# Rates' product of the SSD mixer in plain float32 on the two halves of the array, decay exponents finished on GpSimd, softplus on 128 columns

## The chip, the cores and the metric

The kernel runs on one core of one Trainium2 chip. The metric is the device time of one execution in microseconds, given as the median of several runs; a lower time is better.

## The reference, cut to what matters

The model is a trunk of two layers over 256 tokens of width 2048. Layer 0 mixes tokens with Mamba-2 (SSD), layer 1 with an RG-LRU; each is followed by a SwiGLU FFN and a gated per-layer embedding. The change lies in the SSD mixer of layer 0. Its projection gives, beside z and xBC, one rate per head (64 heads) and token, and the rates give the decays:

```
u = rms_norm(h, norm_mix)
z, xbc, dt = split(u @ in_proj, [4096, 10240])     # dt: the last 64 columns
dt = softplus(dt + dt_bias);  a = -exp(a_log)
a_cs = cumsum(dt * a) within each of the two chunks of 128 tokens
decay_in = exp(where(causal, a_cs[l] - a_cs[s], -inf))
y_diag = einsum(cb, decay_in, xs * dt)             # cb = C . B of a chunk
y_off: the same with the state that chunk 0 leaves for chunk 1
```

There are 8 groups of 8 heads. A head's decays are three 128x128 blocks: chunk 0 with itself, chunk 1 with itself, and chunk 1 against chunk 0 (from the later of whose tokens the state comes).

## The kernel before

**Panels.** Activations lie with features on partitions and the 256 tokens on the free dimension. A weight matrix is walked in panels of 512 output columns. For a panel, `panel` (L226 on) loads raw float32 weights, 512 KB a piece, into a pool of five buffers; `weights` makes of each piece a rounded part `hi` (a cast on ScalarE, L239) and the remainder `lo` (a subtraction on VectorE, L240), four buffers each. For each 128x128 block TensorE multiplies `hi` with 512 columns (the rounded activations and their remainder side by side, L268) and `lo` with 256 columns (L265). For a panel of four blocks the products go in rounds: 16 of `hi`, then 16 of `lo`; four rounds make a panel. All of this is in program order on each engine's own queue as the planner of the framework lays it out; an instruction that waits holds up all behind it on its engine.

**Side work.** After each 12 products `panel` takes one step of a generator in `post` and, by a credit (`pump`, 1.4 steps, 0.6 for two panels of B, 1.35 for the xs panels), one or so of a generator in `side`. Each `yield` ends such a step. So the number of yields sets beside which products a piece of side work is laid.

**The SSD mixer (L382 on)** takes panel 18 (part of C; beside it `load` brings h and scales it into the operands u, which do not yet hold the norm's factor), then the rates' product, panel 19, panels 16 and 17 (B), panels 8 to 15 (xs, one for each group of heads), panels 0 to 7 (z) and the output product. The norm's factor r of each token is made beside panel 19: `bc_part` squares the 16 blocks of h on ScalarE and adds them on VectorE into one accumulator (L176), and `rstd` sums it over partitions with tiny products (L187) and spreads it.

**The rates before.** The weights' 64 columns stand twice side by side in `w_dt`, as two pieces of 512 KB, and go through `panel` like any other, with one block (nb=1): 16 products of `hi` and 16 of `lo`, in which rows 64 to 127 repeat rows 0 to 63. `dt_part` (a side generator) then waits for r, scales, adds the bias, takes softplus (an exp on ScalarE and a series on VectorE) on 128x256, the running sums per chunk into `cs` (128x384: chunk 0, chunk 1 plus chunk 0's total, chunk 1), four transposes (L448), a copy of `cs` to a buffer `sums` in DRAM (96 KB), 29 copies of that row in DRAM (four DMAs, 2784 KB), and then `spread`: for each pair of heads one DMA of 384 KB that gives every partition the pair's running sums (L105; GpSimd masks the two diagonal blocks with affine_select, L403). `move` puts such a DMA on SyncE's queue behind the weight load that was issued last, `last_load`.

**Decays and outputs.** `decays(g)` multiplies B with C (L479, L480), copies that to `cm`, and takes for each head two exps on ScalarE (L88, e<-e,ncs) with minus the token's running sum as the bias, 256 and 128 columns; each pair of heads is then multiplied with `cm` on VectorE (L488). `group(g)` convolves xs, calls `spread` for the next group, takes the steps of `decays(g + 1)`, transposes xs (L507) and makes the outputs: for each head two plain float32 products with 64 weight columns, of 256 and 128 moving columns (L523, L525), heads alternating between rows 0 to 63 and rows 64 to 127 of the bank.

Of the kernel before, what the change touches and what calls it, by code (L numbers as in the profile page):

```python
# [27 lines left out]
COPY = 64 * 384 + 576  # L28
# [16 lines left out]
class Trunk:  # L45
# [120 lines left out]
    def square_add(self, acc, src, first, after=None):  # L166
        nc = self.nc
        q = acc if first else self.tmp.tile([P, T], F32, name="q", tag="q")
        i = nc.scalar.activation(q, src, AF.Square).ins  # L169
        if after is not None:  # L170
            self.tc.add_manual_dep(
                i, after.name,
                mybir.DependencyInfo(mybir.DependencyClass.NoSync, mybir.DependencyReason.DATA),
                reason="not before")
        if not first:
            nc.vector.tensor_tensor(acc, acc, q, ALU.add)  # L176
# [182 lines left out]
    def softplus(self, v, n):  # L359
# [9 lines left out]
        nc.vector.reciprocal(s, s)  # L369
        nc.vector.tensor_tensor(s, s, e, ALU.mult)  # L370
# [12 lines left out]
    def ssd_mixer(self, w_dt, w_in, w_out, load):  # L383
# [7 lines left out]

# [3 lines left out]
        def spread(g, j):  # L395


            e = es[g, j] = pool.tile([P, 2, 384], F32, name="e", tag="e", bufs=8)
            src = sums[0, (g * 8 + 2 * j) * 384:(g * 8 + 2 * j + 2) * 384]
            self.move(e.rearrange("p h c -> p (h c)"),  # L400
                      bass.AP(src.tensor, src.offset, [[COPY, 16], [2 * COPY, 8], [1, 768]]))
            for o in (0, 256):
                nc.gpsimd.affine_select(  # L403
                    out=e[:, :, o:o + P], in_=e[:, :, o:o + P], compare_op=ALU.is_ge, fill=-1e30,
                    base=0, pattern=[[0, 2], [1, P]], channel_multiplier=-1)
# [6 lines left out]
        def bc_part(n, ts, first=None):  # L412
            if first is not None:
                for i in range(0, KT, 4):
                    for k in range(i, i + 4):
                        self.norm_square(k, after=first)
                    yield
# [7 lines left out]
        def dt_part(t):  # L425
            while self.r is None:
                yield
            t = self.scaled(t, self.r)
            v = self.act.tile([P, T], F32, name="dt_v", tag="a")
            nc.vector.tensor_scalar(v, t, self.vec("dt_bias"), None, ALU.add)  # L430
            for dt in self.softplus(v, T):
                yield
# [3 lines left out]
            adt = self.act.tile([P, T], F32, name="adt", tag="a")  # L436
            nc.vector.tensor_scalar(adt, dt, a, None, ALU.mult)
            cs = self.act.tile([P, 384], F32, name="cs", tag="a")

            for c, o in ((0, 0), (1, 256)):  # L440
                nc.vector.tensor_tensor_scan(cs[:, o:o + P], self.ones, adt[:, c * P:(c + 1) * P],
                                             0.0, ALU.mult, ALU.add)
            nc.vector.tensor_scalar(cs[:, P:256], cs[:, 256:], cs[:, P - 1:P], None, ALU.add)
            for _ in range(6):
                yield
            b = self.bank()
            for i, src in enumerate((dt[:, :P], dt[:, P:], cs[:, :P], cs[:, 256:])):
                nc.tensor.transpose(b[:, i * P:(i + 1) * P], src, self.ident)  # L448
            dts = pool.tile([P, 2, P], F32, name="dts", tag="dts", bufs=1)
            ncs = pool.tile([P, 2, P], F32, name="ncs", tag="ncs", bufs=1)  # L450
            nc.vector.tensor_copy(dts, b[:, :256])
            nc.vector.tensor_scalar(ncs, b[:, 256:], -1.0, None, ALU.mult)
            self.dts, self.ncs = dts, ncs
            yield
            yield
            rows = sums[:, :64 * 384]
            self.move(rows[0].rearrange("(h c) -> h c", h=64), cs[:64])
            for _ in range(3):
                yield
            for n in range(1, NCOPY, 8):  # L460
                m = min(n + 8, NCOPY)
                self.move(rows[n:m].rearrange("n (a b) -> n a b", b=1024),
                          rows[0:1].rearrange("n (a b) -> n a b", b=1024).to_broadcast([m - n, 24, 1024]))
                yield
            for _ in range(8):
                yield
            for j in range(NB):
                spread(0, j)
                yield
# [4 lines left out]
        def decays(g):  # L474
# [4 lines left out]
            nc.tensor.matmul(b[:, :256], bt[:, :P], ct, start=True, stop=True, skip_group_check=True)  # L479
            nc.tensor.matmul(b[:, 256:384], bt[:, P:], ct[:, P:], start=False, stop=True, skip_group_check=True)  # L480
            cm = pool.tile([P, 384], F32, name="cm", tag="cm")
            nc.scalar.copy(cm, b[:, :384])
            for n in range(8):
                e, hh, hd = es[g, n // 2], n % 2, g * 8 + n
                self.table(e[:, hh, :256], e[:, hh, :256], AF.Exp, bias=self.ncs[:, 0, hd:hd + 1])
                self.table(e[:, hh, 256:], e[:, hh, 256:], AF.Exp, bias=self.ncs[:, 1, hd:hd + 1])
                if hh:
                    nc.vector.tensor_tensor(e, e, cm.unsqueeze(1).to_broadcast([P, 2, 384]), ALU.mult)  # L488
                yield

        def group(g, ts):
# [23 lines left out]
            def outputs(j):  # L515

                yb = self.bank()
                for i in (j, j + 1):
                    for hh in range(2):
                        e = es[g, i][:, hh, :]  # L520
                        ch = slice(i * P + hh * 64, i * P + hh * 64 + 64)
                        o = yb[hh * 64:hh * 64 + 64, (i - j) * T:(i - j + 1) * T]
                        nc.tensor.matmul(o, xdt[0][:, ch], e[:, :256], start=i == j, stop=False,  # L523
# [360 lines left out]
```

## Time and profile before

| | |
|---|---|
| median of 3 runs | 2684.91 us (2683.16 to 2685.52) |
| the profiled execution's own time | 2682.07 us |
| its span, first to last instruction | 2680.3 us |
| PE busy | 2648.2 us (99%) |
| DVE busy | 1822.4 us (68%) |
| ACT busy | 1501.7 us (56%) |
| POOL busy | 32.5 us (1%) |
| mean granted TensorE clock | 0.996 |
| moved by DMA | 510.77 MB, 191 GB/s |

PE is TensorE's products, PEld its weight loads, DVE VectorE, ACT ScalarE, POOL GpSimd, SP SyncE, on whose queue the DMAs are issued. Times count from the first instruction. "Idle before" in square brackets is the time for which an engine stood still before an instruction, with what released it. PEclk is TensorE's granted clock as a share of the full 2.4 GHz; 0.5 would be 1.2 GHz throughout.

### The profile page before, as it was taken

How to read it: one execution, taken by the hardware profiler on the slowest of the kernel's cores; microseconds unless marked ns; L12 is line 12 of the kernel's file. 1: busy time of each engine (PE TensorE's matmuls, PEld its weight loads, DVE VectorE, ACT ScalarE, POOL GpSimd, SP SyncE). 2: the span in 40 equal slices, each digit the busy share in tenths (PEclk: the TensorE clock that was granted, in tenths of full speed). 3: DMA queues.
4: the chain of work that ended last, by engine and by line, in shares of the span. 5: the costliest groups of instructions: out<-in, count | busy, mean ns of one | idle time of the engine just before them, and what ended most of it. 6: DMA issues, size and time to landing. Idle time of an engine off the chain costs nothing.

```text
span 2680.3 us, 40689 instructions
## 1 busy us (share of the span) xinstructions
PE 2648.2 (99%) x15346; PEld 2334.0 (87%) x15346; DVE 1822.4 (68%) x3066; ACT 1501.7 (56%) x2399; POOL 32.5 (1%) x70
## 2 busy tenths in 40 slices
PE   9899999999999999999999999999999999999998
PEld 7788888888888888888888888888888888888887
DVE  7888878855566655555666899977666555665667
ACT  7677755544444444444455678856444444444555
POOL 0011100000000000000000000000000000000000
PEclk9999999999999999999999999999999999999999
DMA  6767655555555555555655565555555555556553
GB/s 232 244 209 219 190 181 184 186 189 189 184 193 189 189 182 190 195 190 189 194 187 188 172 195 176 196 189 189 189 189 189 196 190 180 189 193 202 186 187 125
DMA packets 141915, 510.77 MB, mean 191 GB/s; under 512 B 15901, under 2 KB 16349, under 8 KB 141661
## 3 DMA queue, kind: packets, MB, share of 16 engines
q1 hardware_dynamic: 141719, 508.18, 57.9%
q8 instruction: 120, 1.97, 0.3%
q14 instruction: 76, 0.62, 0.1%
HBM read 505.92 MB, written 5.05 MB: 191 GB/s over the span
## 4 chain that ended last, share of the span: by engine, by line
PE 90%; DVE 6%; ACT 2%; issue 1%; DMA 1%; SPq 0%; DVEq 0%; ACTq 0%
PE bank L268 58%; PE bank L265 30%; DVE c L356 1%; DVE lo L240 1%; ACT hi L239 1%; DVE t L156 1%; DMA raw<-in_w_ssd_in_dram 1%; PE bank L523 1%; DVE t L163 1%; DVE xc L356 0%; PE bank L625 0%; ACT L88 0%; PE bank L525 0%; PE bank L507 0%; ACT s L153 0%
## 5 line engine op out<-in xcount | busy, mean ns | idle before, releaser
L268 PE MATMUL bank<-x,hi 128*128 128x512 f32 x7360 | 1771.7, 392 | 12.0 <-ACT hi L239 9.9
L268 PEld LDWEIGHTS bank<-x,hi 128*128 128x128 f32 x7360 | 1351.6, 189 | 277.4 <-ACT hi L239 12.7
L239 ACT CAST hi<-raw 128x1024 fp32r<-128x1024 f32 (+1 forms) x932 | 972.1, 1048 | 1031.6 <-PE bank L268 962.6
L240 DVE TENSOR_TENSOR lo<-raw,hi 128x1024 fp32r<-128x1024 f32 (+1 forms) x932 | 1107.2, 1220 | 503.4 <-issue 431.1
L265 PEld LDWEIGHTS bank<-x,lo 128*128 128x128 f32 x7360 | 949.5, 191 | 42.0 <-DVE lo L240 4.8
L265 PE MATMUL bank<-x,lo 128*128 128x256 f32 x7360 | 967.2, 283 | 4.4 <-DVE lo L240 4.4
L156 DVE TENSOR_TENSOR t<-bank,s 128x256 f32<-128x256 f32 x448 | 161.9, 418 | 291.3 <-ACT s L153 290.5
L153 ACT COPY s<-bank 128x256 f32<-128x256 f32 x496 | 160.3, 374 | 13.4 <-PE bank L265 4.8
L163 DVE TENSOR_TENSOR t<-t,r 128x256 f32<-128x256 f32 x216 | 83.2, 427 | 0.0
L356 DVE SCALAR_TENSOR_TENSOR c<-t,vecs,c 128x255 f32<-128x255 f32 (+1 forms) x144 | 63.1, 487 | 0.1
L145 ACT ACTIVATE x<-h,vecs 128x256 fp32r<-128x256 f32 x96 | 47.4, 501 | 17.0 <-DVE h L337 13.8
L88 ACT ACT_TABLE_LOAD x43 | 55.2, 1283 | 1.1 <-DVE c L356 0.3
L337 DVE TENSOR_TENSOR h<-h,t 128x256 f32<-128x256 f32 x144 | 54.2, 420 | 0.2
L146 DVE SCALAR_TENSOR_TENSOR x<-h,vecs,x 128x256 fp32r<-128x256 f32 x96 | 45.5, 480 | 5.9 <-ACT x L145 5.9
L88 ACT ACTIVATE e<-e,ncs 128x256 f32<-128x256 f32 (+1 forms) x128 | 45.3, 442 | 0.1
L176 DVE TENSOR_TENSOR acc<-acc,q 128x256 f32<-128x256 f32 x104 | 43.8, 421 | 2.2 <-ACT q L169 1.4
L169 ACT ACTIVATE q<-h 128x256 f32<-128x256 f32 x104 | 41.4, 405 | 4.7 <-DVE h L337 3.8
L88 ACT ACTIVATE sg<-t 128x256 f32<-128x256 f32 x88 | 32.3, 412 | 18.7 <-DVE t L163 18.7
L137 ACT CAST x<-t 128x256 fp32r<-128x256 f32 x88 | 31.8, 403 | 18.8 <-DVE t L717 18.8
L488 DVE TENSOR_TENSOR e<-e,cm 128x768 f32<-128x768 f32 x32 | 31.0, 970 | 12.6 <-ACT e L88 6.5
L403 POOL TENSOR_SCALAR_AFFINE_SELECT e<-e 128x256 f32<-128x256 f32 x64 | 31.8, 519 | 274.1 <-DMA e<-sums 236.7
L138 DVE TENSOR_TENSOR x<-t,x 128x256 fp32r<-128x256 f32 x88 | 33.3, 421 | 0.0
(121 smaller groups left out, 679.1 us busy)
## 6 DMA issues: line engine op xcount, KB each, us to landing
raw<-in_w_ffn_in_dram SPq DMA_DIRECT2D x352, 512.0 KB, 4.6
raw<-in_w_ffn_out_dram SPq DMA_DIRECT2D x176, 512.0 KB, 4.4
raw<-in_w_ssd_in_dram SPq DMA_DIRECT2D x158, 512.0 KB, 4.5
raw<-in_w_ssd_out_dram SPq DMA_DIRECT2D x64, 512.0 KB, 4.3
raw<-in_w_ple_gate_dram SPq DMA_DIRECT2D x64, 512.0 KB, 4.3
raw<-in_w_lru_in_dram SPq DMA_DIRECT2D x64, 512.0 KB, 4.2
raw<-in_w_lru_out_dram SPq DMA_DIRECT2D x32, 512.0 KB, 4.7
e<-sums SPq DMA_DIRECT2D x32, 384.0 KB, 6.0
```

Of the source, the lines that this page charges most:

```text
L88: i = self.nc.scalar.activation(out, in_, func, **kw).ins
L145: nc.scalar.activation(x[:, :T], src, AF.Copy, scale=w)
L146: nc.vector.scalar_tensor_tensor(x[:, T:], src, w, x[:, :T].bitcast(F32), ALU.mult, ALU.subtract)
L153: nc.scalar.copy(s, b[:, T:])
L156: nc.vector.tensor_tensor(t, b[:, :T], s, ALU.add)
L163: self.nc.vector.tensor_tensor(t, t, r, ALU.mult)
L239: self.last_hi = nc.scalar.copy(hi, src).ins
L240: nc.vector.tensor_tensor(lo, src, hi.bitcast(F32), ALU.subtract)
L265: self.last_product = nc.tensor.matmul(b[:, T:], wt, x[:, :T], start=False, stop=k == nk - 1, skip_group_check=True)
L268: self.last_product = nc.tensor.matmul(b, wt, x, start=k == 0, stop=False, skip_group_check=True)
L337: self.nc.vector.tensor_tensor(hb, hb, t, ALU.add)
L356: nc.vector.scalar_tensor_tensor(out[:, d:], t[:, :T - d], self.vec(cw, (3 - d) * ntap + i), out[:, d:], ALU.mult, ALU.add)
```

## The change

- The rates' product leaves `panel`. `rates` loads the 64 columns once (two pieces of 256 KB into tiles of the activations' pool), multiplies them with norm_mix on VectorE (128x512 each), and multiplies them in plain float32 with h itself, chunk 0 into rows 0 to 63 and chunk 1 into rows 64 to 127 of one bank. The bank is held until r is there.
- So all that follows has 128 columns in place of 256, softplus in more steps; the running sums of a chunk come out of one scan, three transposes take the place of four, and two DMAs (one for each chunk) put them in DRAM, 64 KB in all; the 29 copies are 1856 KB, in four DMAs that lie three steps apart.
- `spread` brings two pairs of heads with one DMA of 512 KB, and GpSimd then does three adds (128x512 each, one with the token's own running sum per block) and two masks of 128x512. There are two spreads for each group in place of four.
- `decays` takes one exp of 128x768 for each pair of heads, with no bias; the product with `cm` and the output products have the same sizes with other strides.
- The squares of the first norm go into two accumulators, of which GpSimd adds one (7 of the adds) and VectorE the other.

```diff
 def square_add(self, acc, src, first, after=None, adder=None):
...
+            (adder or nc.vector).tensor_tensor(acc, acc, q, ALU.add)
 # softplus: two more yields behind the reciprocal and in the series
-            if k == 9:
+            if k in (13, 9, 5):
                 yield
 # spread(g, j), now for j = 0 and 2
+            e = es[g, j // 2] = pool.tile([P, 3, 4, P], F32, name="e", tag="e", bufs=4)
+            n = g * 8 + 2 * j
+            src = sums[0, n * T:(n + 4) * T]
+            self.move(e[:, :2].rearrange("p m h c -> p (m h c)"),
+                      bass.AP(src.tensor, src.offset, [[COPY, 16], [2 * COPY, 8], [1, 4 * T]]))
+            add = lambda m: self.ncs[:, m, n:n + 4].unsqueeze(2).to_broadcast([P, 4, P])
+            nc.gpsimd.tensor_tensor(e[:, 2], e[:, 1], add(2), ALU.add)
+            for m in range(2):
+                nc.gpsimd.tensor_tensor(e[:, m], e[:, m], add(m), ALU.add)
                 nc.gpsimd.affine_select(
+                    out=e[:, m], in_=e[:, m], compare_op=ALU.is_ge, fill=-1e30,
+                    base=0, pattern=[[0, 4], [1, P]], channel_multiplier=-1)
+        def rates():
+            b = self.bank()
+            for i in range(2):
+                w = self.act.tile([P, 8, 64], F32, name="w_dt", tag="a")
+                nc.sync.dma_start(w, w_dt[:, i * 8:i * 8 + 8, :])
+                nc.vector.tensor_tensor(w, w, self.vecs[:, i * 8:i * 8 + 8].unsqueeze(2).to_broadcast([P, 8, 64]),
+                                        ALU.mult)
+                for k in range(8):
+                    for c in range(2):
+                        nc.tensor.matmul(b[c * 64:c * 64 + 64, :P], w[:, k, :],
+                                         self.h[:, i * 8 + k, c * P:(c + 1) * P],
+                                         start=i + k == 0, stop=i + k == 8, skip_group_check=True)
+            return b
 # dt_part(b)
+            for p, c in half:
+                nc.vector.tensor_tensor(v[p], b[p, :P], self.r[p, c], ALU.mult)
+            nc.vector.tensor_scalar(v, v, self.vec("dt_bias"), None, ALU.add)
+            for dt in self.softplus(v, P):
+                yield
...
+            nc.vector.tensor_tensor_scan(cs[:, 0, :], self.ones, adt, 0.0, ALU.mult, ALU.add)
+            nc.vector.tensor_scalar(cs[:64, 1, :], cs[:64, 0, :], -1.0, cs[:64, 0, P - 1:], ALU.mult, ALU.add)
+            for c in range(2):
+                self.move(sums[0, :64 * T].rearrange("(q c h l) -> c q h l", q=16, c=2, h=4)[c],
+                          cs[64 * c:64 * c + 64, 0, :])
+            for _ in range(4):
+                yield
...
             for n in range(1, NCOPY, 8):
+                for _ in range(3):
+                    yield
...
+            for j in (0, 2):
+                for _ in range(3):
+                    yield
                 spread(0, j)
 # decays(g)
-            for n in range(8):
-                e, hh, hd = es[g, n // 2], n % 2, g * 8 + n
-                self.table(e[:, hh, :256], e[:, hh, :256], AF.Exp, bias=self.ncs[:, 0, hd:hd + 1])
-                self.table(e[:, hh, 256:], e[:, hh, 256:], AF.Exp, bias=self.ncs[:, 1, hd:hd + 1])
+            for n in range(4):
+                e = es[g, n // 2][:, :, n % 2 * 2:n % 2 * 2 + 2, :]
+                self.table(e, e, AF.Exp)
+                nc.vector.tensor_tensor(e, e, cm.unsqueeze(2).to_broadcast([P, 3, 2, P]), ALU.mult)
                 yield
 # group(g)
-                if g < 7:
+                if g < 7 and j % 2 == 0:
                     spread(g + 1, j)
...
-            for n in range(5):
-                next(ahead, None)
-                yield
-            yield
+            for n in range(6):
+                if n % 2:
+                    next(ahead, None)
+                yield
 # ssd_mixer
-        self.side.append(dt_part(self.totals(self.panel(w_dt, u, kt=8, nb=1, post=False))[0]))
+        self.side.append(dt_part(rates()))
```

## Rows read from the trace of the kernel before

**Rows 1.** Busy time of each engine by stage: the stretch in us from the span's start and its length, then for each engine its busy time (and instructions), the granted clock, the DMA share and GB/s.
```profile
58.00:83.00 25.00, 20.61 (x111) 18.09 (x111) 23.34 (x50) 17.13 (x27) 0.00 (x0) 0.86 0.37 120
83.00:140.00 57.00, 52.80 (x292) 45.68 (x291) 45.26 (x73) 40.07 (x70) 10.13 (x16) 0.97 0.82 272
140.00:352.00 212.00, 209.78 (x1343) 182.42 (x1342) 183.16 (x297) 161.23 (x291) 21.66 (x48) 1.00 0.66 205
352.00:2667.00 2315.00, 2311.24 (x13314) 2041.25 (x13313) 1520.65 (x2550) 1241.13 (x1945) 0.00 (x0) 1.00 0.57 187
```

**Rows 2.** Timeline of TensorE's products from 30 to 77 us: start, duration, engine, line, operation, count, and the idle time before.
```profile
30.39 3.82 PE L268 MATMUL bank<-x,hi 128*128 128x512 f32 x16
...
35.96 3.82 PE L268 MATMUL bank<-x,hi 128*128 128x512 f32 x16
...
64.45 3.82 PE L268 MATMUL bank<-x,hi 128*128 128x512 f32 x16
72.67 3.78 PE L265 MATMUL bank<-x,lo 128*128 128x256 f32 x16 [4.39 <-DVE lo L240]
76.24 2.64 PE L268 MATMUL bank<-x,hi 128*128 128x512 f32 x9
```

**Rows 3.** Timeline of VectorE from 63 to 73 us, of which these are three.
```profile
63.05 1.75 DVE L369 RECIPROCAL sp<-sp 128x256 f32<-128x256 f32 x1
65.75 0.15 DVE L435 TENSOR_SCALAR a_neg<-a_neg 128x1 f32<-128x1 f32 x1 [0.95 <-ACT a_neg L88]
...
71.39 1.22 DVE L240 TENSOR_TENSOR lo<-raw,hi 128x1024 fp32r<-128x1024 f32 x1
```

**Rows 4.** Groups of instructions by line and shape, over the whole span: busy us, mean ns of one, idle before.
```profile
L403 POOL TENSOR_SCALAR_AFFINE_SELECT e<-e 128x256 f32<-128x256 f32 x64 | 31.8, 519 | 274.1 <-DMA e<-sums 236.7 <-DVE lo L240 25.9 <-DVE t L163 4.9
...
L88 ACT ACTIVATE e<-e,ncs 128x256 f32<-128x256 f32 x64 | 31.8, 497 | 0.1
...
L88 ACT ACTIVATE e<-e,ncs 128x128 f32<-128x128 f32 x64 | 24.8, 387 | 0.0
...
L375 DVE SCALAR_TENSOR_TENSOR sp<-sp,sp 128x256 f32<-128x256 f32 x7 | 3.0, 422 | 0.0
...
L369 DVE RECIPROCAL sp<-sp 128x256 f32<-128x256 f32 x1 | 1.7, 1747 | 0.0
...
L375 DVE SCALAR_TENSOR_TENSOR sp<-sp,sp 128x16 f32<-128x16 f32 x7 | 1.2, 173 | 0.2
...
masks.py:199 POOL TENSOR_SCALAR_AFFINE_SELECT ident<-ident 128x128 f32<-128x128 f32 x1 | 0.3, 292 | 0.1
L369 DVE RECIPROCAL sp<-sp 128x16 f32<-128x16 f32 x1 | 0.2, 248 | 0.0
```

**Rows 5.** Timeline of TensorE's products in the outputs of group 0: two of the four pairs of heads (each float32 product leaves two records).
```profile
159.11 0.65 PE L523 MATMUL bank<-e,xdt 128*64 128x256 f32 x4
...
159.76 0.65 PE L523 MATMUL bank<-e,xdt 128*64 128x256 f32 x4
```

**Rows 6.** Timeline of TensorE's products at the first norm's sum over partitions.
```profile
45.66 0.50 PE L187 MATMUL bank<-ones,acc 128*128 128x1 f32 x4
```

**Rows 7.** Timeline of SyncE's queue, on which DMAs are issued, from 84 to 104 us.
```profile
84.54 2.86 SPq L105 DMA_DIRECT2D sums<-sums  x4
87.93 4.32 SPq L231 DMA_DIRECT2D raw<-in_w_ssd_in_dram  x2
103.37 0.61 SPq L105 DMA_DIRECT2D e<-sums  x1
```

**Rows 8.** Timeline of ScalarE from 104 to 187 us, of which these are three.
```profile
104.60 1.05 ACT L239 CAST hi<-raw 128x1024 fp32r<-128x1024 f32 x1 [4.34 <-DMA raw<-in_w_ssd_in_dram]
...
128.71 4.95 ACT L88 ACTIVATE e<-e,ncs 128x256 f32<-128x256 f32 x14
...
181.07 5.65 ACT L88 ACTIVATE e<-e,ncs 128x256 f32<-128x256 f32 x16
```

**Rows 9.** Timeline of TensorE's products from 105 to 140 us.
```profile
105.70 3.96 PE L268 MATMUL bank<-x,hi 128*128 128x512 f32 x16 [0.58 <-ACT hi L239]
...
117.50 3.01 PE L268 MATMUL bank<-x,hi 128*128 128x512 f32 x12 [0.37 <-ACT hi L239]
120.36 0.59 PE L479 MATMUL bank<-bc,bc 128*128 128x256 f32 x2
...
120.93 1.17 PE L268 MATMUL bank<-x,hi 128*128 128x512 f32 x4
...
129.40 2.00 PE L268 MATMUL bank<-x,hi 128*128 128x512 f32 x8
134.65 3.38 PE L268 MATMUL bank<-x,hi 128*128 128x512 f32 x8 [3.25 <-ACT hi L239]
...
140.06 3.82 PE L268 MATMUL bank<-x,hi 128*128 128x512 f32 x16
```

**Rows 10.** All masks on GpSimd by their line: durations in ns (least/median/most), first and last start in us.
```profile
L403 POOL TENSOR_SCALAR_AFFINE_SELECT e<-e x64: 401/407/1384, 107.9 to 306.6; 128x256 f32<-128x256 f32 x64
```

**Rows 11.** Timeline of GpSimd: the masks of two pairs of heads, two masks each.
```profile
135.26 2.50 POOL L403 TENSOR_SCALAR_AFFINE_SELECT e<-e 128x256 f32<-128x256 f32 x2 [0.19 <-DMA e<-sums]
163.69 0.77 POOL L403 TENSOR_SCALAR_AFFINE_SELECT e<-e 128x256 f32<-128x256 f32 x2 [25.94 <-DVE lo L240]
```

**Rows 12.** Timeline of VectorE beside the first of the rows of GpSimd.
```profile
134.73 4.10 DVE L240 TENSOR_TENSOR lo<-raw,hi 128x1024 fp32r<-128x1024 f32 x3
```

More of the change, by code (lines that the diff above doesn't have):

```diff
@@ L164, in scaled, with square_add @@
         return t
-    def square_add(self, acc, src, first, after=None):
+    def square_add(self, acc, src, first, after=None, adder=None):
         nc = self.nc
@@ L413, in bc_part @@
             if first is not None:
-                for i in range(0, KT, 4):
-                    for k in range(i, i + 4):
-                        self.norm_square(k, after=first)
-                    yield
+                self.acc = [self.tmp.tile([P, T], F32, name="acc", tag="acc") for _ in range(2)]
+                for k in range(KT):
+                    self.square_add(self.acc[k % 2], self.h[:, k, :], k < 2, first, nc.gpsimd if k % 2 else None)
+                    if k % 4 == 3:
+                        yield
                 yield from self.norm_end()
@@ L423, in bc_part, with dt_part @@
                 yield
-        def dt_part(t):
+        def dt_part(b):
             while self.r is None:
                 yield
[L428 to L431, printed above, removed]
+            v = self.act.tile([P, P], F32, name="dt_v", tag="a")
+            half = [(slice(c * 64, c * 64 + 64), slice(c * P, c * P + P)) for c in range(2)]
+            for p, c in half:
+                nc.vector.tensor_tensor(v[p], b[p, :P], self.r[p, c], ALU.mult)
+            nc.vector.tensor_scalar(v, v, self.vec("dt_bias"), None, ALU.add)
+            for dt in self.softplus(v, P):
                 yield
@@ L435, in dt_part @@
             nc.vector.tensor_scalar(a, a, -1.0, None, ALU.mult)
-            adt = self.act.tile([P, T], F32, name="adt", tag="a")
+            adt = self.act.tile([P, P], F32, name="adt", tag="a")
             nc.vector.tensor_scalar(adt, dt, a, None, ALU.mult)
[L438 to L442, printed above, removed]
@@ L443, in dt_part @@
-            nc.vector.tensor_scalar(cs[:, P:256], cs[:, 256:], cs[:, P - 1:P], None, ALU.add)
-            for _ in range(6):
+            yield
+            cs = self.act.tile([P, 2, P], F32, name="cs", tag="a")
+            nc.vector.tensor_tensor_scan(cs[:, 0, :], self.ones, adt, 0.0, ALU.mult, ALU.add)
[3 more added lines that the diff above has]
+                          cs[64 * c:64 * c + 64, 0, :])
@@ L453, in dt_part @@
-            self.dts, self.ncs = dts, ncs
-            yield
[L455 to L459, printed above, removed]
+            nc.tensor.transpose(b[:, :P], dt, self.ident)
+            nc.tensor.transpose(b[:, P:2 * P], cs[:, 0, :], self.ident)
+            nc.tensor.transpose(b[:, 2 * P:2 * P + 64], cs[:64, 1, :], self.ident[:64, :64])
+            dts = pool.tile([P, 2, 64], F32, name="dts", tag="dts", bufs=1)
@@ L461, in dt_part @@
                 m = min(n + 8, NCOPY)
                 self.move(rows[n:m].rearrange("n (a b) -> n a b", b=1024),
[L463 to L467, printed above, removed]
+                          rows[0:1].rearrange("n (a b) -> n a b", b=1024).to_broadcast([m - n, 16, 1024]))
+            for j in (0, 2):
+                for _ in range(3):
+                    yield
```

43 lines of the change are left out of this document (16 added, 27 removed).

## The prediction

> **What bounds the kernel now.** I read the busy times by stage first. From 352 us to the end of the last products TensorE is busy 2311 of 2315 us at the full 2.4 GHz [rows 1]; nothing of the change lies there, and that part can neither give nor lose much. Before 352 us three stages fall short: from 58 to 83 us TensorE is busy 20.6 of 25 us at a mean clock of 0.86, from 83 to 140 us 52.8 of 57, from 140 to 352 us 209.8 of 212 [rows 1]. So the change can win in three ways: fewer columns streamed, fewer stops before 140 us, and the 2.2 us of idle after it. Then I read the timelines of TensorE, to price the stops in rounds. An undisturbed round, 16 hi products and 16 lo products, takes 5.57 us (35.96 less 30.39; that very round is the rates' product) [rows 2]. The round from 64.45 to 76.24 takes 11.79: 4.39 us of idle until VectorE has made lo, then a lo half that lasts 3.57 where an undisturbed one takes 1.9 or so, at the lower clock [rows 1, 2]. Loss 6.2 us. The round from 129.40 to 140.06 takes 10.66, with 3.25 us of idle until ScalarE has cast hi [rows 9]. Loss 5.1 us. Two smaller stops, 0.58 and 0.37, stand before hi at 105.70 and 117.50 [rows 9].
>
> **The change part by part.**
>
> *The rates' product.* Removed: one round, 5.57 us of TensorE [rows 2], with two casts and two subtractions. Added: 16 pairs of plain float32 products, 128 moving columns each, on the two halves. The nearest rows are the outputs, which have the same 64 weight columns: one pair of heads, 256 and 128 columns in each half, goes by in 0.65 us (159.76 less 159.11) [rows 5], so both halves together cost 0.65/3 = 0.217 us for 128 columns. The same 256 and 128 columns in float32 over the whole array, B's product with C, take 0.57 (120.93 less 120.36) [rows 9]. So the halves run side by side there; in turns they would take twice that. 16 x 0.217 = 3.5 us. Net -2.1 us. Upper bound: the halves take turns, because here the order alternates after every product and each brings new weights: 16 x 0.43 = 6.9 us, net +1.4. Lower bound -2.2. I take -2.1, for the outputs alternate after every second product already. The weights' scaling is two operations of 128x512 on VectorE, against two subtractions of twice that size, 1.22 us each [rows 3], now; it is due at 30 us, and its loads are half the bytes of those now, so I cost it at nothing; late, it would cost its own 2.4 us at most.
>
> *The first norm.* Two accumulators need four more records of the tiny product; four now take 0.50 us with the tail [rows 6]: +0.4. One transpose less: -0.1. The adds given to GpSimd take 7 x 0.42 us off VectorE where it does not stop TensorE; if GpSimd is late, r is late, but TensorE takes r only beside panel 19's end. The bank is held longer (from 30 us to r, some 53 us): panels 19 and 16 want eight, so panel 16's last bank waits if VectorE's scaling by r comes after 58 us. Up to +1, taken as 0.
>
> *Softplus and the stop at 72.67.* The lo that TensorE waits for starts at 71.39 on VectorE [rows 3], behind the reciprocal at 63.05, a wait of 0.95 us for ScalarE's a_neg, and five of the seven steps of the series. At 128 columns the reciprocal falls, on the line between its 16 and 256 column rows (248 and 1747 ns) [rows 4], to 0.95 us: -0.80. The series' step falls from 422 ns on the line to 173 at 16 columns to 0.29: -0.13 each, for five of these and some four of their kind -1.2. So lo is ready 2.0 us earlier with the order of VectorE's queue as it is, and idle falls to 2.4. Beyond that, the change puts three more step ends into softplus and one behind it, so that about half of the series is laid behind that lo: another 1 to 2 us. I take 1 us of idle left with the clock kept: 0.58 us of idle costs the next round next to nothing extra (3.96 against 3.82) [rows 9], while 4.39 brings the lower clock. Gain between 0 (the planner's order puts other VectorE work there) and -6.2; I take -4.5.
>
> *The copies and SyncE's queue.* Now no weight load is issued between 92.25 and 103.37: the queue stands behind the first spread, which waits for the copies begun at 84.54 [rows 7]. ScalarE then waits 4.34 us for weights [rows 8], and TensorE stops 0.58 and 0.37 [rows 9]. The copies shrink from 2784 to 1856 KB and lie three steps apart, so only the last one is fresh when a spread asks for it. What is queued behind a spread is weight loads, covered by five buffers of half a round each, 14 us. -0.9, between 0 and -1.3. The two moves of running sums still wait for VectorE's scan as the one does now.
>
> *The exps of group 0 and the stop at 134.65.* ScalarE does 14 exps in a row, 4.95 us, and the casts come only behind them, at 133.66 [rows 8]. A group's 16 exps take 5.65 us. The fixed part is 387 - 128 x 0.86 = 277 ns by the two shapes [rows 4], some 190 ns of it when they follow each other (the rows add to 7.07, the chain takes 5.65, so 89 ns overlap); twelve fewer save 2.3 us. With the casts 2.3 us earlier the idle of 3.25 falls to about 1 and most of the 1.8 us at the lower clock goes. Against that stands GpSimd in front of the exps (below). From -5 to +5; I take -2.3.
>
> *GpSimd.* A spread becomes three adds and two masks of 128x512. A mask costs 292 ns at 128 columns and 407 at 256 [rows 4, 10], so 0.64 at 512. No add on GpSimd is in the trace: with one stream like a mask 0.64, with two streams at the same rate 1.1; the longest mask, 1384 ns for 256 columns [rows 10], bounds it at 2.8. I take 1.1, as it has two inputs. A spread is 3 x 1.1 + 2 x 0.64 = 4.6 us, a group 9.2; by mean against median of the masks (519 to 407, rows 4, 10) beside other work 11.7. What is there for it: the masks of group 2 begin at 163.69 [rows 11], the exps at 181.07 [rows 8], and the second spread's exps 1.7 us later: 19 us. So it fits, and the exps wait for nothing. In the other direction GpSimd slows VectorE: three subtractions took 4.10 us beside masks where three of 1.22 make 3.66, 12% [rows 3, 11, 12]. At 11.7 us a group that is 1.4 us of VectorE in a period of some 27 us (212 us for eight groups), and TensorE already stops 2.2 us there in all [rows 1]. I take +1.0 for groups 0 to 7, from -2 (idle after 140 us gone, with shorter exps) to +8 (1 us for each group).
>
> The Trainium skill speaks against this part: GPSIMD Engine Reference, section 4.1, gives elementwise work with two inputs to VectorE, as about twice as slow on GpSimd, and section 3.1 has 4497 ns for an add of 2048 columns. By an estimate from that an add here would be 1.1 us; the sum is the same by it.
>
> The sum: -2.1 + 0.4 - 0.1 - 4.5 - 0.9 - 2.3 + 1.0 = -8.5 us. The profiled execution took 2682.07 us, 1.8 of it outside its span of 2680.3; with the change 2673.6. The runs' median is 2684.91, 2.8 above the profiled one; against it the forecast is 2676.4 us.
>
> **The rivals.**
>
> *GpSimd in the way (slower).* Beside continuous VectorE work a pair of masks took 2.50 us where 0.77 is usual, 3.2 times [rows 11, 12]. If all of GpSimd's work ran so, a group would take 29 us against 19 and indeed against the 27 us of a group: the exps wait, ScalarE's queue holds the casts behind them, TensorE stops. It decides from 19/9.2 = 2.1 times: below, nothing waits; at 2.6 times the exps come 5 us late, of which the 2.3 us that they became shorter are covered: 2.7 us in each of seven groups, +19 less the gains of 9.5 elsewhere: some 2694. For it: VectorE is busy 86% from 140 to 352 us [rows 1]. Against it: most masks take 407 ns, though VectorE is that busy. 15%.
>
> The same rule stands in the Trainium skill, GPSIMD Engine Reference, section 8: GpSimd shares its SBUF interfaces with VectorE and contends with VectorE instructions of two SBUF inputs. The row of 2.50 us beside three such subtractions agrees.
>
> *The stops move (within 0.2%).* From 58 to 83 us VectorE is busy 23.3 of 25 us [rows 1]. If what it saves only lets the next convolutions in, the stop at 72.67 keeps 2.4 us of idle and the lower clock (-2 in place of -4.5), and group 0's exps wait for GpSimd's masks as long as they became shorter (0 in place of -2.3): the sum is -3.7, 2681. 18%.
>
> *The halves take turns (the change doesn't do what it says).* +1.4 in place of -2.1, the rest as forecast: -5, 2680. 7%, half of it within 0.2%.
>
> *More than forecast.* All stops before 140 us go: -2.1 + 0.3 - 6.2 - 1.3 - 5 = -14, 2671 or, with the idle of the groups, 2668. 12%.
>
> **How the numbers follow.** 0.2% of this time, 5.4 us, is about what a measurement can tell from no change. Forecast 48% (2672 to 2680, of which a few in a hundred come out within 0.2%), more than forecast 12%, stops move 18%, halves take turns 7%, GpSimd slower 15%. Faster: 45 + 12 + 4 = 61%. Within 0.2%: 18 + 3 + 3 = 24%, of which one I give to slower by an added stop. So 0.61, 0.23, 0.16. The range leaves out the outer parts of the slower rival: 2668 to 2690.
>
> **What would show it.** Right: 64 records of the new product in about 3.5 us near 28 us; no idle above 1.5 us before lo near 70 us, and a clock of 1.0 in that stage; no gap of 11 us on SyncE's queue before the first spread; four exps of about 0.85 us in a group, with GpSimd done before them; GpSimd some 90 to 110 us busy. Wrong: exps that wait for GpSimd, or the product at 7 us, or lo still behind softplus.

## The result and the profile after

| | before | after |
|---|---|---|
| median of 4 runs | 2685.22 us (2683.16 to 2687.04) | 2722.97 us (2721.22 to 2723.79) |
| ratio, 95% interval | | 1.014 (1.0122 to 1.0158) |
| profiled span | 2680.3 us | 2719.4 us |

The change made the kernel 38 us slower. The forecast was 2676.4 us in a range of 2668 to 2690, so even the sign was wrong. After the change the first part of the page reads:

```profile
PE 2661.1 (98%) x15381; PEld 2340.2 (86%) x15381; DVE 1844.2 (68%) x3058; ACT 1480.8 (54%) x2300; POOL 91.2 (3%) x93
```

GpSimd's 91.2 us are within the 90 to 110 that the prediction named, and say nothing of a loss. The same stages as in [rows 1] do (columns as there):

```profile
58.00:83.00 25.00, 20.87 (x107) 17.16 (x106) 22.92 (x54) 16.91 (x28) 0.00 (x0) 0.93 0.42 136
83.00:140.00 57.00, 49.29 (x270) 42.98 (x269) 38.29 (x60) 34.84 (x50) 15.81 (x15) 0.91 0.72 224
140.00:352.00 212.00, 188.82 (x1116) 159.33 (x1115) 181.06 (x251) 124.01 (x180) 66.24 (x66) 0.96 0.52 156
352.00:400.00 48.00, 45.19 (x283) 38.60 (x281) 35.25 (x58) 25.30 (x36) 0.00 (x0) 0.96 0.51 169
```

From 140 to 352 us TensorE now idles 23.2 us, where it idled 2.2, and its clock falls to 0.96. VectorE is as busy as before (181.1 against 183.2 us) and gets through 251 instructions in place of 297: it does less in the same time.

To split the 38 us I used the transposes of xs: each group has eight, so their first and last starts bracket seven group periods. The view of that one line, of the kernel before and of the changed one (durations in ns, least/median/most; first and last start in us):

```profile
L507 PE MATMUL bank<-ident,xs x64: 270/272/330, 151.8 to 346.1; 128*128 128x128 f32 x64
```

```profile
L533 PE MATMUL bank<-ident,xs x64: 270/272/475, 153.7 to 385.7; 128*128 128x128 f32 x64
```

The first comes 1.9 us later. From first to last it is 194.3 us before and 232.0 after: 37.7 us more, 5.4 for each period. So the loss lies in the groups, and what the change did ahead of them sums to nearly nothing. That sum has large parts, though. From TensorE's timeline after the change, up to a new stop in panel 17:

```profile
30.00 3.71 PE L424 MATMUL bank<-h,w_dt 128*64 128x128 f32 x64
33.64 3.96 PE L268 MATMUL bank<-x,hi 128*128 128x512 f32 x16
...
63.69 1.22 PE L265 MATMUL bank<-x,lo 128*128 128x256 f32 x8 [1.76 <-DVE lo L240]
...
77.52 2.08 PE L265 MATMUL bank<-x,lo 128*128 128x256 f32 x8 [2.37 <-DVE lo L240]
...
86.62 1.78 PE L268 MATMUL bank<-x,hi 128*128 128x512 f32 x7
...
96.11 3.78 PE L268 MATMUL bank<-x,hi 128*128 128x512 f32 x8 [7.71 <-ACT hi L239]
```

The first `hi` product of each panel starts, before and after, in us: panel 19 35.96 and 33.64, panel 16 58.89 and 57.16, panel 17 88.26 and 86.62, panel 8 111.41 and 118.85, panel 9 140.06 and 141.77. Panel 17, with a new stop of 7.71 us, eats what the front had won.

Now the groups. VectorE's costliest groups from 140 to 352 us, before and after (count | busy us, mean ns | idle before):

```profile
L356 DVE SCALAR_TENSOR_TENSOR c<-t,vecs,c 128x255 f32<-128x255 f32 x32 | 15.6, 508 | 0.0
L356 DVE SCALAR_TENSOR_TENSOR c<-t,vecs,c 128x254 f32<-128x254 f32 x32 | 14.9, 489 | 0.0
...
L163 DVE TENSOR_TENSOR t<-t,r 128x256 f32<-128x256 f32 x32 | 12.9, 462 | 0.0
L156 DVE TENSOR_TENSOR t<-bank,s 128x256 f32<-128x256 f32 x31 | 11.1, 418 | 18.0 <-ACT s L153 17.8
```

```profile
L163 DVE TENSOR_TENSOR t<-t,r 128x256 f32<-128x256 f32 x28 | 23.4, 894 | 0.0
L356 DVE SCALAR_TENSOR_TENSOR c<-t,vecs,c 128x255 f32<-128x255 f32 x28 | 22.1, 809 | 0.0
...
L356 DVE SCALAR_TENSOR_TENSOR c<-t,vecs,c 128x254 f32<-128x254 f32 x27 | 17.9, 684 | 0.0
...
L156 DVE TENSOR_TENSOR t<-bank,s 128x256 f32<-128x256 f32 x28 | 9.9, 416 | 24.4 <-ACT s L153 24.4
```

In the mean the scaling by r (L163) takes nearly twice as long, and the convolutions (L356) up to 1.6 times. The timelines show beside what. GpSimd in the second period, and VectorE beside it:

```profile
169.71 1.04 POOL L406 TENSOR_TENSOR e<-e,ncs 128x512 f32<-128x512 f32 x1 [21.99 <-PE bank L268]
170.70 2.04 POOL L408 TENSOR_TENSOR e<-e,ncs 128x512 f32<-128x512 f32 x2
172.69 1.62 POOL L409 TENSOR_SCALAR_AFFINE_SELECT e<-e 128x512 f32<-128x512 f32 x2
174.28 1.20 POOL L406 TENSOR_TENSOR e<-e,ncs 128x512 f32<-128x512 f32 x1
175.45 2.40 POOL L408 TENSOR_TENSOR e<-e,ncs 128x512 f32<-128x512 f32 x2
177.81 1.59 POOL L409 TENSOR_SCALAR_AFFINE_SELECT e<-e 128x512 f32<-128x512 f32 x2
```

```profile
171.30 1.42 DVE L156 TENSOR_TENSOR t<-bank,s 128x256 f32<-128x256 f32 x4 [2.82 <-ACT s L153]
172.64 3.13 DVE L163 TENSOR_TENSOR t<-t,r 128x256 f32<-128x256 f32 x4
175.69 5.16 DVE L356 SCALAR_TENSOR_TENSOR c<-t,vecs,c 128x255 f32<-128x255 f32 x7
```

From 169.7 to 179.4 GpSimd adds and masks without a break. The DMA that feeds it was issued at 164.84, while the outputs of the group ahead ran (163.19 to 166.1), and landed just before the next group's scaling and convolutions came up on VectorE. Those took 3.13 and 5.16 us; the same four and seven took 1.83 and 3.13 before.

The groups above are means. Taken one by one (each row from a window of its own), these eleven instructions come in three sorts: three beside an add took 1.26 us each, four beside a mask 0.84 or 0.85, and four with no GpSimd instruction beside them 0.42 to 0.47. An add and a mask of GpSimd, and the VectorE instructions beside them:

```profile
174.28 1.20 POOL L406 TENSOR_TENSOR e<-e,ncs 128x512 f32<-128x512 f32 x1
177.81 0.82 POOL L409 TENSOR_SCALAR_AFFINE_SELECT e<-e 128x512 f32<-128x512 f32 x1
```

```profile
174.51 1.26 DVE L163 TENSOR_TENSOR t<-t,r 128x256 f32<-128x256 f32 x1
178.06 0.84 DVE L356 SCALAR_TENSOR_TENSOR c<-t,vecs,c 128x254 f32<-128x254 f32 x1
179.59 0.47 DVE L356 SCALAR_TENSOR_TENSOR c<-t,vecs,c 128x253 f32<-128x253 f32 x1
```

So the masks slow VectorE too, where the adds ahead of them push them beside its work. What that holds up, on ScalarE and then in TensorE's waits over the whole span (us in total, times, longest):

```profile
180.14 1.28 ACT L88 ACT_TABLE_LOAD   x1 [3.03 <-DVE c L356]
...
187.46 0.42 ACT L88 ACTIVATE xs<-c 128x256 f32<-128x256 f32 x1 [0.86 <-DVE c L356]
...
189.19 3.05 ACT L88 ACTIVATE e<-e 128x768 f32<-128x768 f32 x4
```

```profile
PE bank L533 <- ACT xs L88: 16.8, 8, 2.8
PE bank L268 <- ACT hi L239: 13.5, 3, 7.7
PE bank L265 <- DVE lo L240: 12.9, 14, 2.4
```

Late convolutions make late silus (the activation on ScalarE whose result the transposes take), and late silus make late transposes: 16.8 us of stops in eight groups. `lo` comes late behind the convolutions; of its 12.9 us, 8.8 lie between 140 and 400 us, the rest are the two stops ahead of the groups. The exps, four in 3.05 us, stand in that timeline with no wait for GpSimd, and among ScalarE's waits from 100 to 400 us there is none for GpSimd at all.

### The profile page after: what moved, and what is told of

It reads as the page before. It is cut to its first block, busy times and chain, and to the rows that moved or that the text cites. A ratio compares the mean times of both kernels' runs of the same rounds, so it can differ in the third digit from the quotient of the medians.

```text
span 2719.4 us, 40531 instructions
## 1 busy us (share of the span) xinstructions
PE 2661.1 (98%) x15381; PEld 2340.2 (86%) x15381; DVE 1844.2 (68%) x3058; ACT 1480.8 (54%) x2300; POOL 91.2 (3%) x93
## 4 chain that ended last, share of the span: by engine, by line
PE 88%; DVE 6%; issue 1%; ACT 1%; DVEq 0%; ACTq 0%
PE bank L268 57%; PE bank L265 29%; DVE c L356 2%; DVE t L163 1%; DVE lo L240 1%; PE bank L549 1%; DVE t L156 1%; PE bank L651 1%; ACT hi L239 0%; PE bank L551 0%; PE bank L653 0%; PE bank L533 0%; DVE xc L356 0%; PE bank L187 0%; DVE hs L684 0%
## 5 line engine op out<-in xcount | busy, mean ns | idle before, releaser
L265 PE MATMUL bank<-x,lo 128*128 128x256 f32 x7344 | 967.8, 284 | 12.9 <-DVE lo L240 12.9
L156 DVE TENSOR_TENSOR t<-bank,s 128x256 f32<-128x256 f32 x447 | 161.5, 418 | 304.3 <-ACT s L153 303.8
L163 DVE TENSOR_TENSOR t<-t,r 128x256 f32<-128x256 f32 x215 | 94.7, 480 | 0.0
L356 DVE SCALAR_TENSOR_TENSOR c<-t,vecs,c 128x255 f32<-128x255 f32 (+2 forms) x144 | 78.9, 588 | 1.5 <-ACT c L354 1.3
L408 POOL TENSOR_TENSOR e<-e,ncs 128x512 f32<-128x512 f32 x32 | 37.3, 1184 | 0.0
L354 ACT ACTIVATE c<-t,vecs 128x256 f32<-128x256 f32 x48 | 27.8, 596 | 14.7 <-DVE t L163 14.4
L743 DVE TENSOR_TENSOR t<-t,sg 128x256 f32<-128x256 f32 x88 | 33.1, 419 | 0.0
```

The lines of the kernel that those rows point to most:

```text
L156: nc.vector.tensor_tensor(t, b[:, :T], s, ALU.add)
L163: self.nc.vector.tensor_tensor(t, t, r, ALU.mult)
L265: self.last_product = nc.tensor.matmul(b[:, T:], wt, x[:, :T], start=False, stop=k == nk - 1, skip_group_check=True)
L356: nc.vector.scalar_tensor_tensor(out[:, d:], t[:, :T - d], self.vec(cw, (3 - d) * ntap + i), out[:, d:], ALU.mult, ALU.add)
```

## The experiments

The theory: GpSimd's adds, where the change puts them, and the masks behind them make the scaling and the convolutions take up to twice as long in the mean, and these set the groups' period. The rivals: the adds cost wherever they lie; the other parts of the new decays cost (bigger spreads, exps, strides); or the copies do. "First" and "last" are the starts of the first and last transpose, as above.

| run | median us | ratio (95%) | first | last | between |
|---|---|---|---|---|---|
| before | 2685.22 | | 151.8 | 346.1 | 194.3 |
| after | 2722.97 | 1.0122 to 1.0158 | 153.7 | 385.7 | 232.0 |
| e1_old_decays | 2681.25 | 0.9986 to 1.0005 | 156.7 | 350.3 | 193.6 |
| e2_adds_alone | 2712.79 | 1.0103 to 1.0134 | 156.9 | 384.1 | 227.2 |
| e3_adds_for_nobody | 2695.81 | 1.0034 to 1.0064 | 158.2 | 360.6 | 202.4 |
| e4_no_adds | 2689.84 | 1.0015 to 1.0036 | 155.0 | 355.2 | 200.2 |
| e5_six_buffers | 2688.16 | 1.0011 to 1.003 | 154.1 | 351.9 | 197.8 |
| e6_42_tiles | 2722.78 | 1.0134 to 1.0164 | 155.8 | 388.3 | 232.5 |
| e7_no_copies | 2718.57 | 1.0113 to 1.0144 | 148.1 | 383.4 | 235.3 |
| e8_old_decays_no_copies | 2673.96 | 0.9956 to 0.9979 | 141.2 | 339.3 | 198.1 |
| e9_six_buffers_no_copies | 2682.99 | 0.9989 to 1.0007 | 148.3 | 346.2 | 197.9 |
| e10_squares_on_dve | 2675.35 | 0.9961 to 0.9982 | 142.2 | 339.5 | 197.3 |
| e11_before_no_copies | 2676.47 | 0.9968 to 0.9987 | 146.0 | 341.0 | 195.0 |
| e12_old_steps | 2673.85 | 0.9952 to 0.9979 | 140.4 | 336.8 | 196.4 |

Ratios are against the kernel before as run beside each (medians 2682.73 to 2685.22). "First", "last" and "between" come from the one profiled execution of each kernel; it took 4.3 us more than the run's median in e1 and 7.5 more in e2, and lay within 3.2 us of it in the others.

**The old decays with the rest of the change.** `spread`, `decays` and `group` as before, product, squares and softplus as changed; chunk 0's total reaches chunk 1's rows by a small DMA, the copies are 2784 KB again.

```diff
-            nc.gpsimd.tensor_tensor(e[:, 2], e[:, 1], add(2), ALU.add)
-            for m in range(2):
-                nc.gpsimd.tensor_tensor(e[:, m], e[:, m], add(m), ALU.add)
...
+                self.table(e[:, hh, :256], e[:, hh, :256], AF.Exp, bias=self.ncs[:, 0, hd:hd + 1])
+                self.table(e[:, hh, 256:], e[:, hh, 256:], AF.Exp, bias=self.ncs[:, 1, hd:hd + 1])
```

> The changed kernel with the old decays put back: spreads of 384 KB for a pair of heads, two exps with a bias for each head, no adds on GpSimd; the new product, the softplus on 128 columns and the squares stay (the total of chunk 0 goes to the other half of the partitions by a DMA of 64 numbers). Theory (GpSimd's adds slow VectorE's operations of two SBUF inputs, so that the convolutions of groups 1 to 7 come late and TensorE's transposes and lo products with them): the 5 us of each group go, 2680 to 2692, and L163 and L356 are back at some 0.46 and 0.49 us. Rival 1 (exps wait for GpSimd's results): the same total. Rival 2 (the loss comes from the first part, from the product and softplus): above 2710.

Between first and last it took 193.6 us, and from 140 to 400 us the scaling took 479 ns in the mean, the convolutions 471 to 490: the loss is in the new decays. But against before it shows no difference, as a stop of its own took the front's gain. TensorE and ScalarE there:

```profile
108.35 6.25 PE L268 MATMUL bank<-x,hi 128*128 128x512 f32 x16 [11.44 <-ACT hi L239]
```

```profile
107.25 1.04 ACT L239 CAST hi<-raw 128x1024 fp32r<-128x1024 f32 x1 [9.13 <-DMA raw<-in_w_ssd_in_dram]
```

TensorE waits for the cast and the cast for a weight load, one of those issued behind the copies.

**The adds alone.** The kernel before, with two GpSimd adds for each pair of heads and one exp in place of four.

```diff
+            nc.gpsimd.tensor_tensor(e[:, :, :256], e[:, :, :256], add(0, 256), ALU.add)
+            nc.gpsimd.tensor_tensor(e[:, :, 256:], e[:, :, 256:], add(1, P), ALU.add)
...
+                    self.table(e, e, AF.Exp)
```

> The kernel before with one thing alone: GpSimd adds the token's own running sum to a pair's three blocks (128x512 and 128x256 for each spread of 128x768), and ScalarE takes one exp of 128x768 for each pair. Theory: slower by 20 to 45 us, with L163 and L356 at 0.6 us or more beside the adds. Rival 1: slower by as much, with ScalarE's exps waiting for GpSimd in the rows. Rival 2: within 5 us of before.

By the medians it is 30.1 us slower than before, though ScalarE has less to do. In the profiled execution, which took 2720.26 us, 32.9 us more lie between first and last transpose, and the first comes 5.1 later. With that the adds alone bring most of the loss. VectorE from 140 to 352 us:

```profile
L163 DVE TENSOR_TENSOR t<-t,r 128x256 f32<-128x256 f32 x28 | 19.4, 748 | 0.0
L356 DVE SCALAR_TENSOR_TENSOR c<-t,vecs,c 128x254 f32<-128x254 f32 x28 | 18.9, 695 | 0.0
```

**Adds for nobody, and none.** In both the third block comes by a DMA of its own. The first adds and masks into a scratch tile, fed by a small DMA; the second has only the masks.

```diff
 # e3_adds_for_nobody
-            nc.gpsimd.tensor_tensor(e[:, 2], e[:, 1], add(2), ALU.add)
+            self.move(e[:, 2], bass.AP(src.tensor, src.offset + 4 * P, [[COPY, 16], [2 * COPY, 8], [1, 4 * P]]))
+            self.move(tick, bass.AP(src.tensor, src.offset, [[COPY, 16], [2 * COPY, 8], [1, 4]]))
+            nc.gpsimd.tensor_tensor(s, q, add(2), ALU.add)
 # e4_no_adds: the second line, and of the adds none
```

> The changed kernel, with the same three adds and two masks for each spread, but on a scratch tile that nobody reads; they start when a small DMA behind the spread's has landed. The exps read what the DMAs brought (the third block by a second DMA of 256 KB), so the token's own sum and the masks are left out of the result. The activations' pool has 47 tiles in place of 48. Theory: as slow as the changed kernel, 2710 to 2730, with L163 and L356 slow. Rival 1: 2680 to 2692, as no exp waits for GpSimd.

> The changed kernel without the adds: GpSimd only masks, the third block comes by a second DMA of 256 KB; the token's own sum is left out of the exponents. Theory: the 5 us of each of groups 1 to 7 go, 2680 to 2695. Rival 3 (the new places of the steps and the one large exp make the loss): above 2710.

Without adds 2689.8: with the masks of 128x512 alone most of the loss is gone (200.2 us between; convolutions 517 to 521 ns in the mean from 140 to 400 us). With adds that nobody waits for 2695.8, which lies in neither range named for e3: 6.0 us over e4, not 30. I had meant e3 to tell "contention" from "waiting for GpSimd", and it did so badly, for its adds run at other times: fed by the small DMA they run from 163.47 to 175.2 us in one period whose scaling comes at 181.45 only. From 140 to 352 us VectorE's scaling took 551 ns in the mean there and its longest convolutions 509. That raised the question of the place, which the next run answers.

**The place alone.** Two more buffers for the decays let the spread go out before the outputs of the group ahead. The buffers' space comes from the activations' pool; the second run takes that space and does nothing with it.

```diff
 # e5_six_buffers
-        self.act = pool("act", 48)
+        self.act = pool("act", 42)
-            e = es[g, j // 2] = pool.tile([P, 3, 4, P], F32, name="e", tag="e", bufs=4)
+            e = es[g, j // 2] = pool.tile([P, 3, 4, P], F32, name="e", tag="e", bufs=6)
 # e6_42_tiles: the first pair of lines alone
```

> The changed kernel with six buffers for the decays in place of four, so that a group's spread need not wait for the outputs of the group two before it, and GpSimd's adds fall beside the end of the panel before in place of the next group's convolutions; the activations' pool shrinks from 48 to 42 tiles to make room. Nothing else is changed, the adds are as many. Theory (it is the place of the adds beside the convolutions that costs; adds for nobody that fell beside other VectorE work cost 6 us): 2685 to 2700, L163 and L356 below 0.6 us. Rival (adds cost the same wherever they fall, and those for nobody were cheap only because they read less): 2715 to 2725.

> The changed kernel with 42 tiles in the activations' pool and nothing else, the control for the six buffers. Either theory: within 5 us of the changed kernel, 2718 to 2728.

The same adds, laid elsewhere: 34.8 us less than after, 197.8 us between first and last. The smaller pool changes nothing (2722.8). VectorE's groups with six buffers, 140 to 352 us, and GpSimd and VectorE in one period:

```profile
L240 DVE TENSOR_TENSOR lo<-raw,hi 128x1024 fp32r<-128x1024 f32 x64 | 87.0, 1371 | 0.0
L514 DVE TENSOR_TENSOR e<-e,cm 128x768 f32<-128x768 f32 x29 | 28.0, 1025 | 0.0
L356 DVE SCALAR_TENSOR_TENSOR c<-t,vecs,c 128x255 f32<-128x255 f32 x32 | 14.6, 476 | 0.0
...
L163 DVE TENSOR_TENSOR t<-t,r 128x256 f32<-128x256 f32 x32 | 13.7, 488 | 0.0
```

```profile
191.53 1.04 POOL L406 TENSOR_TENSOR e<-e,ncs 128x512 f32<-128x512 f32 x1 [16.19 <-DMA e<-sums]
192.53 4.00 POOL L408 TENSOR_TENSOR e<-e,ncs 128x512 f32<-128x512 f32 x2
...
200.67 1.22 POOL L409 TENSOR_SCALAR_AFFINE_SELECT e<-e 128x512 f32<-128x512 f32 x2
```

```profile
192.10 3.54 DVE L240 TENSOR_TENSOR lo<-raw,hi 128x1024 fp32r<-128x1024 f32 x2
...
203.33 2.84 DVE L356 SCALAR_TENSOR_TENSOR c<-t,vecs,c 128x255 f32<-128x255 f32 x7
```

GpSimd is done at 201.9, and the convolutions start behind it at full speed. Beside the adds lie subtractions now, up to 2.06 us each in place of 1.22 (1371 ns in the mean), and TensorE stops for `lo` only once from 140 to 400 us, for 0.4 us.

**Without the copies.** All partitions read row 0 of `sums`; the 29 copies go. Four kernels got this edit: the changed one (shown), e1, e5 and the kernel before, the second and the last with the sizes of the old decays.

```diff
-                      bass.AP(src.tensor, src.offset, [[COPY, 16], [2 * COPY, 8], [1, 4 * T]]))
+                      bass.AP(src.tensor, src.offset, [[0, 16], [0, 8], [1, 4 * T]]))
...
-                self.move(rows[n:m].rearrange("n (a b) -> n a b", b=1024),
-                          rows[0:1].rearrange("n (a b) -> n a b", b=1024).to_broadcast([m - n, 16, 1024]))
```

> The changed kernel without the 29 copies in DRAM: every partition's spread reads the one row. Theory for the stop of 7.7 us before the hi at 96 us (weight loads that are queued behind the copies, and casts that the planner lays late for it): the stop goes, 2712 to 2716. Rival (VectorE's softplus and convolutions hold the casts): the stop stays, 2720 or more. If reading one row 128 times is slow, the spreads land later than 6 us and exps wait: 2725 or more.

> The kernel with the new product and softplus and the old decays, without the 29 copies: the stop of 11.4 us near 97 us, in which ScalarE waits 9.1 us for a weight load behind the copies, goes, and the total is 2666 to 2674, faster than both kernels. Rival (the stop only moves, or single-row reads are slow): 2678 or more.

> The changed kernel with six buffers for the decays, 42 tiles in the activations' pool, and without the 29 copies. Theory (two separate losses: adds beside the convolutions, and the stop of 7.7 us with the lower clock that hangs on the copies): 2688 less 7 to 10, 2678 to 2682, some 0 to 5 us faster than the kernel before. Rival (without the copies GpSimd's adds of group 0 come to lie elsewhere and give the gain back, as without the copies alone only 4 us were gained): 2684 to 2688.

> The kernel before without the 29 copies and with nothing of the change. If the new product and softplus are worth nothing, and the gain of the old decays without copies is the copies' alone, it stands at 2674, too. If they are worth the 1.9 us of the product and something of the stop at 72.67 us: 2677 to 2682.

The first transpose comes 5.6, 15.5, 5.8 and 5.8 us earlier, in that order. (Of the 15.5, 1.7 stand before the rates' product, which starts at 32.62 in e1's profile and at 30.92 in e8's.) In the changed kernel most of it is given back between (235.3 us), so the total moves 4.4 us only, to 2718.57, between its two ranges; with the old decays (e8) 7.3 us stay, and that version beats both kernels. With both losses mended (e9) the change only draws level with the kernel before (2682.99 us, just over the range of its theory) and stays 9.0 us behind e8; as the groups take as long in both (197.9 and 198.1 us), and the first transpose comes 7.1 us later in e9, that lies ahead of the groups. Why, no run shows. The kernel before without copies (e11) falls between its two ranges. In e8 the stop behind the copies is gone; its stage from 83 to 140 us:

```profile
83.00:140.00 57.00, 57.00 (x332) 50.50 (x331) 48.10 (x81) 42.07 (x75) 10.18 (x16) 1.00 0.78 240
```

**Two parts of what is left.** In e8, once the squares' adds all on VectorE, once softplus with its old steps.

```diff
 # e10_squares_on_dve
-                    self.square_add(self.acc[k % 2], self.h[:, k, :], k < 2, first, nc.gpsimd if k % 2 else None)
+                    self.square_add(self.acc[k % 2], self.h[:, k, :], k < 2, first)
 # e12_old_steps, of whose lines the first stands behind the reciprocal
-        yield
...
-            if k in (13, 9, 5):
+            if k == 9:
```

> The new product and softplus with the old decays and no copies, and the seven adds of squares back on VectorE (the two accumulators stay). Theory (GpSimd's adds of the squares cover nothing that TensorE waits for): within 3 us of 2674. Rival (they unload VectorE in front of the stop at 64 us): 2677 or more; or they slow VectorE: 2671 or less.

> The new product and softplus with the old decays and no copies, and softplus in its old steps (without the two added step ends). If the steps ease the stop near 64 us, as the prediction had it: 2677 or more, with over 2.5 us of idle before that lo. If the halved columns alone do: within 2 us of 2674.

Neither differs from 2673.96 by more than its interval. In e12 the stop near 64 us is 1.75 us, with all steps 1.76; in e11, with 256 columns and the old product, it is 4.39 at 73.09. So the added step ends in softplus do nothing for that stop, and what shortens it is the fewer columns or the new product; no run parts these two.

## Why the prediction was wrong

*The step that failed* is the GpSimd term, "+1.0 for groups 0 to 7, from -2 to +8". It measured +37.7 us in the groups (e2 shows 30.1 for the whole kernel with the adds alone, and e5 takes 34.2 back by moving them). The step rested on "three subtractions took 4.10 us beside masks where three of 1.22 make 3.66, 12%". That sum leaves out that one subtraction starts before the last has ended: three undisturbed take 3.49 us, so the row shows 17%. But the larger fault is what I carried it to. The row was of long subtractions beside masks; short instructions beside adds lost far more, the scaling by r 894 ns in place of 462 in the mean, 93%. The trace of the kernel before shows some of it already, and the prediction doesn't use it: beside masks of 128x256 a convolution took up to 657 ns, where 476 is the median.

```profile
123.08 3.49 DVE L240 TENSOR_TENSOR lo<-raw,hi 128x1024 fp32r<-128x1024 f32 x3
```

```profile
L356 DVE SCALAR_TENSOR_TENSOR c<-t,vecs,c x96: 466/476/657, 141.7 to 342.5; 128x255 f32<-128x255 f32 x32, 128x254 f32<-128x254 f32 x32, 128x253 f32<-128x253 f32 x32
```

And I spread the loss over VectorE's whole period as if any of its work were alike, when the adds fell on the very instructions that the transposes wait for. The prediction asked whether GpSimd would be ready for the exps; it didn't ask what VectorE would be doing in the 10 us when GpSimd works. Nor was the place hidden: the masks of group 2 begin at 163.69 [rows 11], and VectorE's scaling and first convolutions of that period ran from 167.85 to 172.7 before.

*The slower rival* had the wrong mechanism. No exp waits for GpSimd, and GpSimd's own time was forecast well: an add took 1.04 us in the clear (1.1 forecast) and 1.16 to 1.18 in the mean, and the work for a group 9.7 us in the second period (9.2 to 11.7 forecast), where the rival needed over 19. GpSimd slows VectorE more than VectorE slows it there.

Of TensorE's loss from 140 to 400 us, 26.0 us are idle (23.2 + 2.8), against 2.2 and next to nothing [rows 1]; the lower clock, 0.96 over 260 us, is worth some 10 more by estimate from the windows.

*The rates' product* was right: 64 records in 3.64 us (33.64 less 30.00), 3.5 forecast. The halves run side by side, and the rival in which they take turns falls.

*The norm's sums and transposes* took 0.6 (panel 19 starts 2.32 us earlier, panel 16 1.73), 0.3 forecast. *Softplus, -4.5*, was worth nothing in the changed kernel: panel 17 starts 1.64 us earlier, no more than the product and the norm give. The stop at 72.67 became two, 1.76 at 63.69 and 2.37 at 77.52. That is the rival "the stops move", in its first half; its reason, that what VectorE saved went to the convolutions and to the order of its queue, is argued and not shown. Without the copies and with the old decays the front is worth more: the first transpose comes at 141.2 in e8 and at 146.0 in e11, 4.8 us, of which the medians keep 2.5.

*The copies, -0.9*, became +9.1: panel 8 starts 7.44 us late where panel 17 was 1.64 early. The new stop of 7.71 us before `hi` at 96.11 goes with the copies (e7 has no idle from 83 to 140 us). That it hangs on them is shown. On ScalarE's queue the four casts start at 95.03, right behind a silu that had waited 1.65 us for a convolution, and no load is waited for; why the casts lie behind the silus with the copies and between them without stays open.

*The exps of group 0, -2.3*, became -5.7 by panel 9's start (7.44 late, then 1.71): the stop at 134.65 is gone.

What stays open: why part of the front's gain is given back between the transposes when the copies go (e8 3.8 us against before, e7 3.3 against after), and what the last 3.5 us of e5's groups are.

The version to keep is e8: 0.9967 of before (0.9956 to 0.9979). Most of its gain comes without any of the change, by leaving out the copies (e11, 2676.47); product, softplus and squares together add some 2.5, with intervals that overlap; by the timeline the product's net is 1.9 of it.

## What to carry to other kernels

Before work goes to GpSimd, lay its time slot beside VectorE's timeline: if instructions with two SBUF inputs that TensorE will wait for lie there, count each at its own time and most of one GpSimd instruction more (here 0.8 us beside an add, 0.4 beside a mask), so that many short ones lose most; if none lie there, the same work may be nearly free. Such a slot is set by when a buffer comes free, so one more buffer can be worth more than the work itself. And a share of 3% busy says nothing of what an engine does to its neighbour.

## What the runs showed of the hardware

Beside GpSimd's work VectorE's instructions with two SBUF inputs went in step with GpSimd's, one of each: in the second period five of them in a row started at 174.51, 175.69, 176.87, 178.06 and 178.82, and GpSimd's at 174.28, 175.45, 176.63, 177.81 and 178.58. So what such an instruction lost went by the GpSimd instruction beside it: a convolution of 0.47 us took 1.26 beside an add and 0.84 beside a mask, and a scaling of 0.42 took 1.26 and 0.85. The means of 894 and 809 ns mix these. The same engine's L156, of the same size as the scaling with one input in the bank and one in SBUF, kept 416 ns, even at 171.30, in the midst of the adds. Which engine loses more goes by the lengths: beside the short instructions an add took 1.20 us in place of 1.04, while beside subtractions of 128x1024 in e5 (up to 2.06 us in place of 1.22) two adds took 4.00 in place of 2.04.

The Trainium skill, GPSIMD Engine Reference, section 8, says that GpSimd shares its SBUF interfaces with VectorE and contends with VectorE instructions of two SBUF inputs. The runs agree, L156 included, and give it a size.

A spread in which all partitions read one row of DRAM landed in 6.6 to 8.2 us in the median, against 5.9 to 7.7 with 30 rows to read (0.5 to 1.1 us later in each of the four pairs of kernels). That is all that the copies bought in these runs; up to the first transpose they cost 5.6 to 5.8 us in three of the pairs and up to 15.5 in the fourth.
